# Experts of a mixture-of-experts layer run four at a time in column tiles, their tokens fetched as rows from DRAM

## The chip, the core and the metric

The kernel runs on one core of one Trainium2 chip. The core has a matrix engine (TensorE, "PE" in the profile, with its weight loads as "PEld"), a vector engine ("DVE"), a scalar engine ("ACT"), GpSimd ("POOL") and a sync engine ("SP") that mostly issues DMAs. All data are 32-bit floats. The metric is the device time of one execution in microseconds (us), as the median of several runs.

## The reference

Two transformer-like blocks run over 512 tokens of 1024 columns. The last part of the second block, the only one that the change touches, is a hierarchical mixture of experts: each token chooses one of 8 groups and in it 2 of 8 experts. Cut to what matters:

```python
x = x + merged @ w_out
h2 = rms_norm(x, norm2_g).reshape(b * s, d)
...
expert_id = g_sel[:, None] * 8 + top_i                 # two experts of 64 for each token
gate = p_group[:, None] * jax.nn.softmax(top_v, axis=-1)
...
def expert_block(args):                                 # d_model 1024, d_ff 256
    xb, e = args
    hid = jax.nn.silu(xb @ w_gate_e[e]) * (xb @ w_up_e[e])
    return hid @ w_down_e[e]
...
return x + jnp.zeros_like(h2).at[tok].add(ys * wt[:, None])
```

There are 1024 assignments of a token to an expert, and each expert's three matrices are 1 MiB each, 192 MiB for all 64.

## The kernel before

The two blocks up to the output projection are one long stream of dense products on PE; they end near 1590 us and are the same in both kernels. What follows is the expert part, in this order in the program.

*Routing.* `ev_out2` runs once for each of four blocks of 128 tokens: it adds the output projection to x (kept in four tiles `xt[m]`, token rows), takes the row's 1/rms, transposes the block for the router's logits and ranks the tokens within their experts (`Rk`: the place of a token in its expert's list, or a negative number). Each expert has a block of 32 token places (CAP); two experts with more than 32 tokens are put last and get a second block each (N_SPARE = 2). Any further ones would follow in a loop, which makes no pass with these inputs. The tokens of the first four experts are collected within `ev_out2` already, by products with one-hot columns added up in two banks that `gather_open` sets to zero: a memset on POOL (L1582) and a product of it on PE (tile `xqT<-zero`).

*Weights.* `load_w` loads one matrix into one slab of 1 MiB by one DMA from SP (L1859). There are 16 slabs; `pump_w(limit)` issues loads ahead until `limit` slabs are in use, and `drop_w` gives a slab back. The limit is 13 for the first two experts, then 12, then 11, since the sums (`acc`) take two slabs. The matrices of one expert lie in the buffers of the dense products' pieces. From expert 24 on the order of the experts is found at run time.

*Fetching tokens.* For each group of 8 experts `select` and `gates` build one-hot matrices (token, place) `S` and the same times the gates, `gate_rows` brings the gates along a row, and `gather_k` multiplies x with `S` on PE, in 8 chunks of 4 products, giving the tokens transposed (`xsT`, 1024 columns on partitions, 256 places). ACT and DVE evict the chunks in turn.

*One expert.* `gate_up` runs 16 products of 128x32 by 128x256 in four column tiles of PE (two halves of K, gate and up) and ACT copies the 128x256 result (`part`). `hidden` adds the halves and transposes by two products with a constant "i2"; ACT takes a tanh, DVE three small products (L2062 to L2064, the last one with the row of gates). `down` runs 8 products of 128x32 by 128x256, four column tiles for four quarters of the output. `expert_out` brings the four quarters to their places: four ACT copies (L2086, the high part) and four DVE subtractions (L2088, the low part), 32x256 each.

*Adding up.* For each four experts `scatter_mat` builds a one-hot (place, token) matrix `ST` (DVE `sel` L2105, one product, DVE L2109) and `combine` multiplies it with the high and low parts of the output, 8 times 2 products of 512 columns, and DVE adds each to `acc` (L2123). After the last group each half block is stored by SP (L2343).

*Order.* All engines run in program order. A table in the code (`todo`, `early`, filled by `at`) says ahead of which expert each step of fetching, scattering and adding is emitted, so that PE has such work between the products of an expert that depend on each other. All products are recorded at the helper's line, L114, and the shape of the tiles tells them apart. An instruction of PE shows as two records where the data are 32-bit (16 products of `gate_up` as x32).

Of the kernel before, what the change touches and what calls it, by code (L numbers as in the profile page):

```python
# [10 lines left out]
F32 = mybir.dt.float32  # L11
# [9 lines left out]
P = 128  # L21
T = 512
# [14 lines left out]
def const_arrays():  # L37
    """Constants that follow from the shapes."""
# [15 lines left out]
    i2 = np.zeros((P, P))  # L54
    for r in range(P):
        i2[r, r % 64] = 1.0
    add("i2", i2)
# [22 lines left out]
def layer_kernel(ctx, tc, A, out, dbg=None, stop=None):  # L80
# [96 lines left out]
    def rsqrt_steps(v, scale, res):  # L177
        """Steps towards two [P, 1] factors (appended to res) whose product is scale/sqrt(v)."""
# [13 lines left out]
    def alternate(*lists):  # L192
        """Run the steps of some chains in turn."""
# [5 lines left out]
    def split(hi, lo, src, scale=None):  # L199
        """src (f32) as the exact sum of two float32r tiles."""  # L200
# [7 lines left out]
    def split_later(hi, lo, src, scale=None, lag=0):  # L208
        """split, the engines' parts emitted one after the other."""
# [14 lines left out]
    class Pair:  # L224
        """hi/lo slabs of an activation laid out [128, kc, n]; chunks from `extra` on lie in m2 tiles."""
# [20 lines left out]
    class Ref:  # L246
        """Stands for a Pair that is made later."""

    def diag(r, r2=None):
        """diag(r), or diag(r * r2)."""  # L250
# [7 lines left out]
    def scaled(xap, f):  # L258
        """Rows times their two factors, in place."""
# [6 lines left out]
    def sum_squares(xh):  # L266
        """Sums of squares of the rows of some halves of 512."""
# [6 lines left out]
    def rstd_steps(xh, res, ss=None):  # L274
        """Steps towards two factors of 1/rms of the rows given as two halves of 512."""
# [77 lines left out]
    class Step:  # L353
        """run() emits the products, yielding after each few (a piece when it is done with that one)."""
# [9 lines left out]
    def ws_steps(wap, K, c0, ncols, ref, evac):  # L364
        """out^T tiles [128 columns, T] of pair^T @ w[:, c0:c0+ncols]; evac(j, ps)."""
# [39 lines left out]
    def xs_steps(wap, c0, ref, nm_blocks, evac):  # L405
        """out [128 tokens, 512] of pair @ w[:, c0:c0+512], K = 1024; evac(m, ps)."""
# [24 lines left out]
    def narrow_step(wap, c0, ref, evac):  # L431
        """out^T [32, T] of pair^T @ w[:, c0:c0+32], K = 1024."""
# [15 lines left out]
    def full_steps(wap, K, ref, evac, hold=True):  # L448
        """out [T tokens, 1024] of pair @ w; evac(m, [ps0, ps1]). Uses every PSUM bank."""
# [40 lines left out]
        if hold:  # L490
            # the third block's evacuation waits until the next weights are under way
# [49 lines left out]
    def pump_lows(upto=None):  # L541
        """Emit the low parts of pieces prepared in an earlier quantum, and all up to piece `upto`."""
# [33 lines left out]
    def run_steps(n, rate=0.0):  # L576
        """Emit the next n dense steps, with `rate` background ticks per 24 products."""
# [41 lines left out]
    def pipeline(units):  # L619
        """units: lists of (lag in quanta, function); one unit starts per tick."""  # L620
# [1796 lines left out]
```

## Time and profile before

| | |
|---|---|
| runs, us | 2151.99, 2151.8, 2159.45 (median 2151.99) |
| profiled execution, span | 2155.4 us, 31387 instructions |
| its own time | no other than its span is given; the span is 3.4 us above the median |
| PE busy | 2063.3 us (96%) |
| DVE / ACT / POOL busy | 1251.3 (58%) / 839.4 (39%) / 83.9 (4%) |
| first expert's product to the end | 1608.3 to 2155.4 us |

The profile page gives busy time per engine over the whole span, then the span in 40 slices of 53.9 us. The change touches only what lies behind about 1570 us, that is the last 11 slices, so the whole-span shares say little about it; windows, waits and the timeline of that part say more. "Busy" of PE is modelled from the ends of matmuls. The granted clock of TensorE is given as a share of its full 2.4 GHz; 0.5 is the lower level.

### The profile page before, as it was taken

The numbers are of one execution on the slowest core, as the hardware profiler recorded it, in microseconds if no ns is written. First come the engines' busy times: TensorE is split into PE (matmuls) and PEld (weight loads), VectorE is DVE, ScalarE is ACT, GpSimd is POOL, SyncE is SP. The second block draws the span as 40 slices with busy tenths as digits, with TensorE's granted clock in tenths as the row PEclk, the third lists the DMA queues.
The fourth block names the chain that finished last, engine by engine and source line by source line (L and its number), as shares of the span: only waits on it lengthen the run. The fifth ranks groups of instructions, "written<-read, shape, count | busy, mean of one in ns | idle before, by whom it ended". The sixth has DMA issues, their size and how long they took to land.

```text
span 2155.4 us, 31387 instructions
## 1 busy us (share of the span) xinstructions
PE 2063.3 (96%) x12321; PEld 1611.6 (75%) x12322; DVE 1251.3 (58%) x2820; ACT 839.4 (39%) x1747; POOL 83.9 (4%) x94
## 2 busy tenths in 40 slices
PE   7999999999999999989999999999999889989996
PEld 6777788888888888766687888888887656657664
DVE  5445436437665623878755887584354555665555
ACT  5443323325444422535533655552213333333322
POOL 3000000001000000211010000000000000000000
PEclk9999999999999999999999999999999999999998
DMA  9522232354112352301113242342747999999992
GB/s 229 192 84 69 79 98 79 108 176 157 45 54 78 132 191 88 110 20 42 54 45 127 89 137 79 108 116 90 256 170 271 346 391 372 418 389 368 418 378 98
DMA packets 164406, 363.59 MB, mean 169 GB/s; under 512 B 17706, under 2 KB 116338, under 8 KB 140064
## 3 DMA queue, kind: packets, MB, share of 16 engines
q1 hardware_dynamic: 157536, 341.31, 43.6%
q0 software_dynamic: 6720, 20.25, 3.4%
q8 instruction: 98, 1.61, 0.3%
q14 instruction: 52, 0.43, 0.1%
HBM read 355.15 MB, written 9.00 MB: 169 GB/s over the span
## 4 chain that ended last, share of the span: by engine, by line
PE 65%; DVE 8%; ACT 2%; issue 1%; ACTq 0%; POOL 0%; POOLq 0%
PE ws L114 30%; PE full L114 7%; PE xsT L114 6%; PE gu L114 5%; PE down L114 3%; PE xs L114 3%; PE cmb L114 2%; PE xqT L114 1%; DVE ys L2088 1%; PE hid L114 1%; PE yps L114 1%; DVE acc L2123 1%; ACT ys L2086 1%; PE o L114 1%; PE ssc L114 1%
## 5 line engine op out<-in xcount | busy, mean ns | idle before, releaser
L114 PE MATMUL ws<-hTh,wh 128*128 128x512 f32 x1152 | 467.6, 406 | 0.5 <-ACT q2T L1073 0.5
L346 DVE TENSOR_TENSOR wl<-raw,wh 128x1024 fp32r<-128x1024 f32 x230 | 283.8, 1235 | 308.2 <-ACT wh L339 306.7
L114 PE MATMUL ws<-hTh,wl 128*128 128x512 f32 x1152 | 449.5, 390 | 0.0
L114 PE MATMUL ws<-hTl,wh 128*128 128x512 f32 x1152 | 449.4, 390 | 0.0
L339 ACT ACTIVATE wh<-raw 128x1024 fp32r<-128x1024 f32 x247 | 259.1, 1053 | 233.0 <-PE ws L114 106.5
L114 PEld LDWEIGHTS ws<-hTh,wh 128*128 128x128 f32 x1152 | 216.3, 188 | 63.0 <-issue 17.7
L114 PEld LDWEIGHTS ws<-hTh,wl 128*128 128x128 f32 x1152 | 216.2, 188 | 46.8
L114 PEld LDWEIGHTS ws<-hTl,wh 128*128 128x128 f32 x1152 | 216.6, 188 | 42.9 <-issue 2.2
L691 DVE SCALAR_TENSOR_TENSOR cv<-ws,pcol,cv 128x510 f32<-128x510 f32 (+1 forms) x152 | 113.8, 749 | 115.7 <-ACT cv L689 112.6
L2088 DVE TENSOR_TENSOR ys<-down,ys 32x256 fp32r<-32x256 f32 x264 | 111.0, 421 | 114.8 <-ACT ys L2086 111.8
L2086 ACT ACTIVATE ys<-down 32x256 fp32r<-32x256 f32 x264 | 98.8, 374 | 191.8 <-PE down L114 189.3
L114 PE MATMUL xsT<-S,x 128*128 128x256 f32 (+2 forms) x512 | 139.3, 417 | 0.8 <-ACT S L1969 0.8
L114 PEld LDWEIGHTS xsT<-S,x 128*128 128x128 f32 x512 | 126.9, 334 | 13.0 <-issue 8.9
L114 PE MATMUL gu<-we,xsT 128*32 128x256 f32 x1856 | 117.7, 397 | 0.0
L114 PE MATMUL cmb<-ys,ST 128*128 128x512 f32 x264 | 95.2, 458 | 5.0 <-DVE ys L2088 3.5
L114 PEld LDWEIGHTS gu<-we,xsT 128*32 128x32 f32 x1856 | 64.3, 115 | 43.9 <-issue 8.9
L114 PE MATMUL down<-we,hid 128*32 128x256 f32 x1056 | 75.2, 407 | 21.9 <-DVE hid L2064 15.6
L2123 DVE TENSOR_TENSOR acc<-acc,cmb 128x512 f32<-128x512 f32 x120 | 80.6, 684 | 25.2 <-PE cmb L114 23.9
L689 ACT ACTIVATE cv<-ws,pcol 128x512 f32<-128x512 f32 x64 | 49.7, 776 | 108.6 <-PE ws L114 108.6
L114 PEld LDWEIGHTS down<-we,hid 128*32 128x32 f32 x1056 | 29.5, 113 | 56.7 <-DVE hid L2064 21.2
L114 PE MATMUL xs<-wh,hTh 128*128 128x512 f32 x160 | 66.2, 414 | 1.8 <-ACT wh L339 1.7
L114 PE MATMUL xs<-wl,hTh 128*128 128x512 f32 x160 | 64.0, 400 | 2.6 <-DVE wl L346 2.6
(544 smaller groups left out, 3284.9 us busy)
## 6 DMA issues: line engine op xcount, KB each, us to landing
we<-in_w_gate_e SPq DMA_DIRECT2D x63, 1024.0 KB, 10.2
we<-in_w_up_e SPq DMA_DIRECT2D x63, 1024.0 KB, 8.6
we<-in_w_down_e SPq DMA_DIRECT2D x63, 1024.0 KB, 9.9
raw<-in_w_in SPq DMA_DIRECT2D x56, 1024.0 KB, 5.3
raw<-in_w_up SPq DMA_DIRECT2D x22, 1024.0 KB, 5.2
raw<-in_w_down SPq DMA_DIRECT2D x11, 1024.0 KB, 6.4
raw<-in_w_out SPq DMA_DIRECT2D x8, 1024.0 KB, 4.9
AC<-acum_d POOLq DMA_DIRECT2D x16, 512.0 KB, 4.9
```

The costliest lines, as they stand in the source:

```text
L114: pe.matmul(o, l, r, start=start, stop=stop)
L339: act.activation(hi, src, AF.Copy)
L346: eng.tensor_tensor(lo, src, hi.bitcast(F32), op=ALU.subtract)
L689: act.activation(a, src, AF.Identity, scale=taps[0], bias=bias)
L691: dve.scalar_tensor_tensor(a[:, lag:], src[:, :T - lag], taps[lag], a[:, lag:], op0=ALU.mult, op1=ALU.add)
L2086: act.activation(hi[32 * j:32 * j + 32, a], dp[32 * q:32 * q + 32, :], AF.Copy)
L2088: dve.tensor_tensor(lo[32 * j2:32 * j2 + 32, a], dp[32 * q:32 * q + 32, :], hi[32 * j:32 * j + 32, a].bitcast(F32), op=ALU.subtract)
L2123: dve.tensor_tensor(o_, o_ if gs[0] else xt[m][:, c], ps, op=ALU.add)
```

## The change

Routing, ranking, the weights and the arithmetic of the experts stay. What is different:

- `ev_out2` also stores each block of x to a third DRAM tile, by a DMA from POOL.
- The experts go in groups Q of four (15 of four, one of two, and one with two blocks for each of the last two experts). `pair` does gate and up of two experts in the four column tiles, all eight parts of K in one sum; `hidden` transposes with two products per pair and does not multiply by gates; `down` runs four experts in the four column tiles, 16 products of 512 columns into two banks.
- `group_out` evicts 128 rows at once, two ACT and two DVE instructions of 512 columns, with the gate as a scale for each row.
- The tokens of the next group are fetched as rows: `slots` builds the one-hot of 4 x 32 places, `table` gets gate, token number and 1/rms for each place by four products of 6 columns and four small DVE operations, `fetch` issues an indirect DMA from POOL with the token numbers (an empty place has a number out of range and is skipped), and `turn` scales the rows on ACT, transposes them with eight products and evicts them by one DVE and four ACT instructions.
- `combine` adds into the tiles of x, so `acc` is gone and 13 slabs are for weights throughout. The three matrices of expert 3 (not 1) lie in the buffers of the pieces. The order of the weights is gate and up of two experts, gate and up of the next two, then the four down matrices.
- The table of the order is replaced by one loop over the groups.

```diff
     def ev_out2(m, pss):
...
         for x_, p_ in zip(xh, pss):
             dve.tensor_tensor(x_, x_, p_, op=ALU.add)
+        gp.dma_start(x_d[2][m * P:(m + 1) * P, :], xap)
...
-    E_SMALL, N_FIRST = 1, 10
-    w_order = [(e, i) for e in range(last[0]) for i in range(3) if e != E_SMALL]
...
+    E_SMALL, N_FIRST, N_LIVE = 3, 10, 13
+    w_order = []
+    for e in range(0, N_EXP, 2):
+        w_order += [(e + j, i) for j in range(2) for i in range(2)]
+        if e >= 4 * N_Q:
+            w_order += [(e + j, 2) for j in range(2)]
+        elif e % 4:
+            w_order += [(e - 2 + j, 2) for j in range(4)]
...
+    def table(Q):
+        w_, S = width(Q), sel_S[Q]
+        tp = bank((P, 6), "tab")[0:w_]
+        for m in range(NM):
+            mm(tp, S[:, m, :], Gx[:, m, min(Q, N_Q), :], start=m == 0, stop=m == NM - 1)
...
+    def fetch(Q):
+        w_ = width(Q)
+        xg[Q] = pieces.tile([P, D], F32, tag="wh", name=nm("xg"))[0:w_]
+        gp.indirect_dma_start(out=xg[Q], out_offset=None, in_=x_d[2],
+                              in_offset=bass.IndirectOffsetOnAxis(ap=slot[Q][2], axis=0),
+                              bounds_check=T - 1, oob_is_err=False)
+
+    def turn(Q):
+        w_, x_ = width(Q), xg.pop(Q)
+        act.activation(x_, x_, AF.Copy, scale=slot[Q][1])
+        t = pieces.tile([P, 8, w_], F32, tag="wl", name=nm("xT"))
+        for b in range(2):
+            ps = bank((P, 4, w_), "xT")
+            for k in range(4):
+                pe.transpose(ps[:, k, :], strided(x_, 4 * b + k), ident[0:w_, 0:w_])
...
-    def gate_up(xc, wts):
+    def gate_up(xcs, wts):
         gu = bank((P, 256), "gu")
-        for k4 in range(4):
-            for q in range(4):
-                kh, ch = q // 2, q % 2
-                k = 4 * kh + k4
-                mm(gu[32 * q:32 * q + 32, :], xc(k), wts[ch](k), start=k4 == 0, stop=k4 == 3)
+        for k in range(8):
+            for q in range(4):
+                mm(gu[32 * q:32 * q + 32, :], xcs[q // 2](k), wts[q](k), start=k == 0, stop=k == 7)
...
-    def down(hid, wd):
-        dp = bank((P, 256), "down")
-        for f in range(2):
-            for q in range(4):
-                mm(dp[32 * q:32 * q + 32, :], hid[:, f, :], wd(f)[:, 256 * q:256 * q + 256],
-                   start=f == 0, stop=f == 1)
-        return dp
+    def down(hids, wds):
+        dps = [bank(name="down") for _ in range(2)]
+        for h in range(2):
+            for f in range(2):
+                for j, wd in enumerate(wds):
+                    mm(dps[h][32 * j:32 * j + 32, :], hids[j // 2][:, f, j % 2, :], wd(f)[:, h * T:(h + 1) * T],
+                       start=f == 0, stop=f == 1)
+        return dps
...
+    for Q in range(N_Q + 1):
+        whole = Q < N_Q
+        part = pair(Q, 0, 4 * Q)
+        ready(Q + 1)
+        if Q == 0:
+            rank_cols()
+            table(0)
+        else:
+            combine(Q - 1, range(2))
+        hids = [hidden(part)]
+        if whole:
+            part = pair(Q, 2, 4 * Q + 2)
...
+        if Q:
+            combine(Q - 1, range(2, NM))
+        scatter_mat(Q)
+        if whole:
+            hids.append(hidden(part))
+        turn(Q + 1)
+        second(Q, hids, [4 * Q + j for j in range(4 if whole else 2)])
```

(`ready` is slots, table and fetch of a group; `second` is down and `group_out`; `pair` and `second` give back their slabs and issue further loads.)

PE late in the expert part, from the last combining products ahead of an expert's down to it. In a row stand the line, the operation, the output and the operands. Before, one expert:

```order
L114 MATMUL cmb_16973<-ys_16541,ST_16693 128x512
L114 MATMUL cmb_16973<-ys_16542,ST_16693 128x512
L114 MATMUL hid_16977<-ca,part_16958 128x128 x2
L114 MATMUL xsT_16985<-S_16439,x_12143 128x128 x2
L114 MATMUL xsT_16985<-S_16442,x_12144 128x128 x2
L114 MATMUL cmb_17001<-ys_16541,ST_16693 128x512
L114 MATMUL cmb_17001<-ys_16542,ST_16693 128x512
L114 MATMUL ST_17005<-RkT_13656,sel_17006 128x512
L114 MATMUL down_17011<-we_16733,hid_16980 32x256 x8
```

After, a group of four experts, ending with the first five of 16 down products:

```order
L113 MATMUL cmb_13730<-ys_13586,ST_13530 128x512
L113 MATMUL cmb_13730<-ys_13587,ST_13530 128x512
L113 MATMUL ST_13735<-RkT_13293,sel_13736 128x512
L2023 MATMUL hid_13740<-ca,part_13708 128x128 x2
L1992 MATMUL xT_13749<-ca,xg_13648 128x128 x4
L1992 MATMUL xT_13755<-ca,xg_13648 128x128 x4
L113 MATMUL down_13764<-we_13512,hid_13671 32x512
L113 MATMUL down_13764<-we_13578,hid_13671 32x512
L113 MATMUL down_13764<-we_13580,hid_13743 32x512
L113 MATMUL down_13764<-we_13582,hid_13743 32x512
L113 MATMUL down_13764<-we_13512,hid_13671 32x512
```

Before, fetching and combining products stand between an expert's hid and its down; after, the transposes of the next group's fetched rows (xg) stand there, and the down products read the hid of both pairs.

POOL from the start of routing (x_12144 and x_12145 are the tiles of two token blocks each, x_d_93 the third DRAM tile). Before:

```order
L1828 MEMSET routing_12149 128x8x24
L1833 DMA routing_12149<-in_norm_g 128x8
L1582 MEMSET zero_12601 128x512
L2195 MEMSET ov_15528 128x2
L2346 TENSOR_LOAD nx_15562
```

After:

```order
L1826 MEMSET routing_12150 128x8x24
L1831 DMA routing_12150<-in_norm_g 128x8
L1535 DMA x_d_93<-x_12144 128x1024 x2
L1535 DMA x_d_93<-x_12145 128x1024 x2
L1580 MEMSET zero_12606 128x512
L1980 DMA xg_12803<-x_d_93,ix_12798 128x1024
L1980 DMA xg_12983<-x_d_93,ix_12978 128x1024
```

The memset for the zero product now stands behind four stores of x, and the fetches of the groups (16 in all) behind it.

DVE late in the expert part. Before, what stands in a row for one expert:

```order
L2105 CAST sel_17494<-ca 64x128
L2109 TENSOR_SCALAR ST_17497<-ST_17493,ca 128x512
L2088 TENSOR_TENSOR ys_17509<-down_17499,ys_17508 32x256 x4
L2062 SCALAR_TENSOR_TENSOR hid_17540<-hid_17540,hid_17537 128x64
L2063 TENSOR_TENSOR hid_17540<-hid_17540,hid_17537 128x64
L2064 TENSOR_TENSOR hid_17540<-hid_17540,grow_17174 128x64
L2123 TENSOR_TENSOR acc_13245<-acc_13245,cmb_17545 128x512
```

After, from the second pair's hid of one group to the slot operations of the next:

```order
L2027 SCALAR_TENSOR_TENSOR hid_13539<-hid_13539,hid_13536 128x128
L2028 TENSOR_TENSOR hid_13539<-hid_13539,hid_13536 128x128
L1994 TENSOR_TENSOR xT_13544<-xT_13545,routing_12150 128x512
L2054 SCALAR_TENSOR_TENSOR ys_13587<-down_13560,slot_13210,ys_13586 128x512
L2054 SCALAR_TENSOR_TENSOR ys_13587<-down_13561,slot_13210,ys_13586 128x512
L1958 TENSOR_TENSOR S_13635<-routing_12150,ca 128x512
L1969 TENSOR_TENSOR slot_13642<-tab_13637,ca 128x4
L1970 TENSOR_REDUCE slot_13642<-slot_13642 128x1
L1972 TENSOR_SCALAR ix_13643<-tab_13637 128x1
L1973 COPY slot_13642<-tab_13637 128x1
```

Four evictions per expert have become two per four experts, and the numbers of the rows to fetch (ix) come out of four small operations that stand behind the one-hot S.

## Rows read from the trace of the kernel before

**Rows 1.** The page: span; busy us, share, instructions; GB/s of 40 slices.

```profile
span 2155.4 us, 31387 instructions
...
PE 2063.3 (96%) x12321; PEld 1611.6 (75%) x12322; DVE 1251.3 (58%) x2820; ACT 839.4 (39%) x1747; POOL 83.9 (4%) x94
...
GB/s 229 192 84 69 79 98 79 108 176 157 45 54 78 132 191 88 110 20 42 54 45 127 89 137 79 108 116 90 256 170 271 346 391 372 418 389 368 418 378 98
```

**Rows 2.** Windows: us, busy of PE PEld DVE ACT POOL, clock, DMA share, GB/s.

```profile
1620.00:1660.00 40.00, 39.18 (x346) 31.70 (x349) 17.90 (x49) 13.11 (x36) 0.00 (x0) 1.00 0.70 263
...
1820.00:1860.00 40.00, 38.05 (x347) 28.17 (x347) 20.79 (x52) 13.29 (x37) 0.00 (x0) 1.00 1.01 418
```

**Rows 3.** Waits from 1620 (PE) and 1500 (SP): waiter, releaser, sum us, count, longest.

```profile
PEld down L114 <- DMA we<-in_w_up_e: 1.0, 4, 0.2
...
PE down L114 <- DVE hid L2064: 15.6, 13, 3.9
...
SPq L1859 <- PE down L114: 288.9, 59, 9.9
SPq L1859 <- PE gu L114: 105.7, 60, 19.3
```

**Rows 4.** Groups by form from 1620 us: busy us, mean ns, then idle before.

```profile
L2088 DVE TENSOR_TENSOR ys<-down,ys 32x256 fp32r<-32x256 f32 x264 | 111.0, 421 | 114.8 <-ACT ys L2086 111.8
L114 PE MATMUL xsT<-S,x 128*128 128x256 f32 x384 | 105.6, 419 | 0.8 <-ACT S L1969 0.8
...
L2123 DVE TENSOR_TENSOR acc<-acc,cmb 128x512 f32<-128x512 f32 x120 | 80.6, 684 | 25.2 <-PE cmb L114 23.9
...
L114 PE MATMUL hid<-ca,part 128*128 128x128 f32 x260 | 43.8, 292 | 0.6 <-ACT part L2050 0.6
```

**Rows 5.** The chain that ended last: start us, length us, engine, work, records.

```profile
1571.20 0.88 PE h2T L1520 x8
...
1774.20 1.86 PE down L114 x16
...
1790.46 1.07 PE down L114 x16
1791.53 1.73 PE gu L114 x32
...
2113.91 1.85 PE cmb L114 x8
```

**Rows 6.** Timeline from the routing to the first experts: start, length, engine, instruction, [idle before].

```profile
1567.15 0.52 POOL L1582 MEMSET zero<- 128x512 bf16 x1 [38.95 <-issue]
...
1588.17 0.39 PE L114 MATMUL xqT<-zero,routing 128*128 128x512 bf16 x1
...
1589.13 1.28 DVE L1535 TENSOR_TENSOR x<-x,full 128x512 f32<-128x512 f32 x2
...
1608.34 4.52 PE L114 MATMUL gu<-we,xqT 128*32 128x256 f32 x64
...
1611.16 0.33 SPq L1859 DMA_DIRECT2D we<-in_w_up_e  x1
```

**Rows 7.** DMA issues: count, KB each, us from issue to landing.

```profile
we<-in_w_down_e SPq DMA_DIRECT2D x63, 1024.0 KB, 9.9
...
dsk<-in_d_skip POOLq DMA_DIRECT2D x2, 4.0 KB, 18.6
```

**Rows 8.** Timeline of SP at the end: the last weights and the stores of the output.

```profile
2100.63 2.04 SPq L1859 DMA_DIRECT2D we<-in_w_down_e  x2
...
2137.16 7.70 SPq L2343 DMA_DIRECT2D out<-acc  x8
```

**Rows 9.** A window with a low clock, and the ST product in it and later.

```profile
1770.00:1780.00 10.00, 7.73 (x58) 3.67 (x58) 5.60 (x14) 2.15 (x7) 0.00 (x0) 0.66 0.99 401
...
1773.44 0.76 PE L114 MATMUL ST<-RkT,sel 64*128 64x512 f32 x1 [2.27 <-DVE sel L2105]
...
1833.98 0.49 PE L114 MATMUL ST<-RkT,sel 64*128 64x512 f32 x1 [1.34 <-DVE sel L2105]
```

More of the change, by code (lines that the diff above doesn't have):

```diff
@@ L53, in const_arrays @@
     add("swa", np.where(np.concatenate([prev_ok, own_ok], 1), 0.0, 8.0 * NEG))
[L54 to L57, printed above, removed]
+    add("m4", 0.5 * (p[:, None] // 32 == np.arange(4)[None, :]))
+    add("m2", 0.5 * (2 + p[:, None] // 32 % 2 == np.arange(4)[None, :]))
     add("iota32", np.broadcast_to(np.arange(32), (P, 32)))
@@ L743, in pairs_of @@
         return [t[j] for i in range(0, len(lists[0]), 2) for t in lists for j in (i, i + 1) if j < len(t)]
-    x_d = [drp.tile([T, D], F32, name=f"x_d{i}") for i in range(2)]
+    x_d = [drp.tile([T, D], F32, name=f"x_d{i}") for i in range(3)]
     nxt = {}
@@ new lines, in slots @@
+    def slots(Q):
+        S = sel_S[Q] = m2((P, NM, width(Q)), name="S")
+        n = 4 if Q < N_Q else 2
+        e0 = 4 * Q if Q <= N_Q else N_EXP - N_SPARE
+        sh = [P, NM, n, CAP]
+        for i in range(1 if Q <= N_Q else 2):
+            s = S.rearrange("p m (r e s) -> p m r e s", e=n, s=CAP)[:, :, i]
+            dve.tensor_tensor(s, Rk[:, :, e0:e0 + n, None].to_broadcast(sh),
+                              C("iota64")[:, None, None, CAP * i:CAP * i + CAP].to_broadcast(sh), op=ALU.is_equal)
@@ L2051, in gate_up, with hidden @@
         return part
-    def hidden(part, gr):
+    def hidden(part):
         cp = bank((P, 2, P), "hid")
@@ L2322, in second_half @@
-    def second_half(e, hid):
-        dp = down(hid, weights(e, 2))
-        pump_w(limit(e))
-        expert_out(e, dp)
-    part = None
-    for e in range(N_EXP - N_SPARE):
-        this = part or gate_up_of(e)
-        part = gate_up_of(e + 1) if e < N_AHEAD else None
-        second_half(e, first_half(e, this))
-    hids = []
-    for e in range(N_EXP - N_SPARE, N_EXP):
-        two = [(b, gate_up_of(b)) for b in (e, e + N_SPARE)]
-        hids += [(b, first_half(b, part)) for b, part in two]
@@ L2336, in layer_kernel, with xcol @@
-    for b, hid in hids:
-        second_half(b, hid)
-    assert not todo and not early
-    for m in range(NM):
-        for h in range(2):
-            c = slice(h * T, (h + 1) * T)
-            combine([G4 - 1, G4], m, h)
-            sp.dma_start(out[0, m * P:(m + 1) * P, c], acc[m // 2][:, m % 2, c])
+    group_gates()
+    group_tokens()
+    sel_S[0] = moe["q"][0][0]
+    order, prep = order_prep(), overflow_prep()
+    def xcol(Q, j):
+        return lambda k: xT[Q][k // 4][:, k % 4, 32 * j:32 * j + 32]
@@ new lines, in pair, with second @@
+    def pair(Q, j, e, last=True):
+        part = gate_up([xcol(Q, j), xcol(Q, j + 1)], [ew[e + b, i] for b in range(2) for i in range(2)])
+        if last:
+            for b in range(2):
+                for i in range(2):
+                    drop_w(e + b, i)
+            pump_w(N_LIVE)
+        return part
+    def second(Q, hids, es):
+        dps = down(hids, [ew[e, 2] for e in es])
+        for e in sorted(set(es)):
+            drop_w(e, 2)
+        pump_w(N_LIVE)
+        group_out(Q, dps)
@@ new lines, in ready @@
+    def ready(Q):
+        slots(Q)
+        table(Q)
+        fetch(Q)
+    for Q in range(N_Q + 1):
[5 more added lines that the diff above has]
+            table(0)
+        else:
+            combine(Q - 1, range(2))
+        hids = [hidden(part)]
+        if whole:
+            part = pair(Q, 2, 4 * Q + 2)
+        if Q in (1, 2):
+            next(order, None)
+            next(order, None)
+        if Q in (8, 9, 10, 11):
+            next(prep, None)
+        if Q:
+            combine(Q - 1, range(2, NM))
[4 more added lines that the diff above has]
+        second(Q, hids, [4 * Q + j for j in range(4 if whole else 2)])
@@ L2346, in layer_kernel @@
+    Q, e = N_Q + 1, N_EXP - N_SPARE
+    part = pair(Q, 0, e, last=False)
+    combine(Q - 1, range(2))
+    hids = [hidden(part)]
+    part = pair(Q, 2, e)
+    combine(Q - 1, range(2, NM))
+    scatter_mat(Q)
+    hids.append(hidden(part))
+    second(Q, hids, [e, e + 1, e, e + 1])
+    assert wnext["i"] == len(w_order) and not ew and next(order, None) is None and next(prep, None) is None
+    combine(Q, range(NM), store=True)
     nov = nc.values_load(ov["n"][0:1, 0:1], min_val=0, max_val=MAXBLK)
```

295 lines of the change are left out of this document (84 added, 211 removed).

## The prediction

> **What bounds the kernel now.** I read the page's head, busy shares and GB/s line first [rows 1]: one core, span 2155.4 us, PE 96% busy; only in the last quarter does the GB/s line come up to 418. The experts run from 1608 us to the end, so everything below is about some 547 us. I then cut that part into windows [rows 2]: at 1820 to 1860 the queues carry 418 GB/s at a share of 1.01 and PE is busy for 38 of 40 us; at 1620 to 1660 PE is busy for 39.2 and the queues move only 263 GB/s. Two things are near their end at once, and the waits tell which one paces [rows 3]: PE waited 1.0 us in all for a weight, while the weight queue on SP waited 289 + 106 us for PE's products to leave a slab. So PE paces, and the DMA idles behind it in the parts below 418.
>
> The floor of the other side: 64 experts have 192 matrices of 1 MiB [rows 7]. Sixteen are issued before the first slab is free (13 slabs, three in the buffers of the dense products); the other 176 are 184.5 MB, at 418 GB/s 441.5 us. Before issues them from 1611 to 2102 [rows 6, 8], 491 us: 33.5 us for every twelve, that is for four experts.
>
> **The change part by part.**
>
> *PE, per four experts.* After, gate/up has as many products as before: 4 × 1.73 = 6.9 us at the full clock [rows 5]. Down has half the instructions at twice the width; at equal columns it is the old 4 × 1.07 = 4.3, with 3.5 as the other end if some of the old time was start-up; I take 4. Combining stays 8 × 2 products of 0.23 (eight took 1.85) = 3.7. The one-hot products that fetched tokens go: 105.6 us for the 384 of six groups of eight [rows 4], 8.8 for each four experts; in their place come 8 transposes, 0.88 like the eight h2T [rows 5], 4 table products of 6 columns (a 292-ns hid product is the nearest above [rows 4], so 0.2 to 1.2), an ST of 0.5 [rows 9] and 4 hid transposes below 1.2. Sum about 17 to 18 us; with some 3 us of waits inside (before waited 15.6 us in 13 places for hid [rows 3], 1.2 each; here two hid chains and the turn of the fetched rows) 21, against before's 33.5.
>
> *DVE and ACT, per four.* Before, 16 evictions of 421 ns and 8 adds of 684 [rows 4], the hid operations and part of the token evictions; after, 2 evictions of 512 columns (684 bounds one), 4 hid operations, 8 adds of 684, 4 small slot operations and one 512-wide xT: 11 us on DVE where about 20 stood. ACT falls likewise. Neither nears 30 us.
>
> *DMA, per four.* 12 matrices = 12.58 MB, 30.1 us at 418 GB/s. The fetches are new: 1024 token places less the 47 of the first four experts, by the reference's router, are 977 rows of 4 KB = 4.0 MB, 9.6 us in all if they only take bytes; unused slots are skipped (if they moved bytes as well, 8 MB, 19 us). So a group needs 30.7 us of the queues and 21 of PE: **the queues become the bound**, if the slabs hold enough of a lead. All 13 stay with weights (before: 13, 12, then 11), and nine matrices are in flight or landed while PE works on a pair, 22 us of stream.
>
> *The new wait on POOL.* ev_out2 now stores each x block to DRAM from POOL, ahead of gather_open's memset. Before, the memset ran at 1567.15, long before need, and PE's zero product at 1588.17 [rows 6]. Now it is queued behind the last block's store, which waits for the DVE adds ending 1590.4; the issue is put at 0.5, as long as the memset's 0.52, so PE's zero product stands at about 1591.5: 3.3 us later, on the path, with the routing behind it. The lower bound is 0 (if routing's other chain hides it), the upper 4. I take 3.3. The last store's half MB is 1.3 us of the queues at 418 GB/s, and the weights' queue stands still until 1611 [rows 6], so that costs nothing; under a full stream it would cost those 1.3.
>
> *The sum.* First gate/up 1608.3 + 3.3 = 1611.6; two experts 4.5 at the clock found there, so the first slabs are free at 1616.2. A gap while the first groups run through their lead: 0 to 8 us, since the lead covers 22; I take 0. Stream 441.5 + fetch 9.6 + 2 for the last landing: last weight at 2069 to 2070. After it, PE has the second pair's gate/up, combining and hid of the last four blocks partly undone: last down lands some 5 us after the last gate/up; from then gate/up 3.45 × 2, combining 1.85 × 2, hid chain 2 to 3 put the down at T + 8.5, its 4 us, 2.2 for evictions, 8 adds of 0.684 to T + 20, and from the last store's issue to the end 10.5 as before (2144.9 to 2155.4 [rows 8]): T + 31. Before took 52.7 us from its last weight's issue to the end [rows 8], and its queues stood empty for most of it. End: 2070 + 31 = 2101 of span, against 2155.4: −54.7. The profiled execution is 3.4 us above the median of 2151.99; taken off, **2097 us**.
>
> **The rivals.**
>
> A, above: the queues set the pace. For it: 418 GB/s holds over 40 us while PE computes [rows 2], and in two slices of 54 us of the page [rows 1]. Bounds: no fetch cost, 3.3 hidden, and a tail of 25 give 2079; a starting gap of 8, every row moved and a tail at half clock (+7) give 2112.
>
> B, the clock. In A, PE idles 10 us in 31, in gaps before each pair and each down. The rows show what a gap does: after 2.27 us idle the ST product of 64 x 512 took 0.76, and 16 down products 1.86, against 1.07 later; the window's clock was 0.66 [rows 5, 9]. After 1.34 us idle the same ST took 0.49 [rows 9]. At half clock a group needs 34 to 37 us, more than the stream; but then the gaps close and the clock comes back (before runs at 1.00 with few gaps), so I expect 31.5 to 34 per group: 15 × 0.8 to 3.3 more, 2109 to 2147. The Trainium skill, "TensorE: Matmul & The Clock Gate", HAM oscillation, describes just this: compute shorter than the wait for the next transfer starts every burst cold; held to the letter, all groups at 37 would end near 2192, but such groups leave no gap.
>
> C, the stream is slower than 418. The page's slices from 1670 us to the last two lie at 346 to 418 [rows 1], with PE pacing; rows fetched at scattered addresses may cost more than their bytes. At 372, 188.5 MB take 507, not 451: 2153, **no change**. The Trainium skill, "DMA: Bandwidth & Descriptors", Specifications, gives an HBM limit of about 358 GB/s per core: by it the stream would take 527 and the end be near 2172. The trace disagrees with 418 [rows 1, 2].
>
> D, slower: the fetch's latency. Indices for group Q+1 are ready only after PE's table products in group Q, and turn, before Q's down, needs the rows; PE's down is queued behind turn. The slowest POOL transfers of the trace, two small ones, took 18.6 us [rows 7]. With F from index to landing, a group cannot be shorter than F and what lies on that circle besides: scaling the rows 1, transposes 0.9, their evictions 2, down 4, the next gate/up 3.5, table and slot operations 1.2, in all 12.6 + F. It sets the pace from F = 18.1; 15 groups reach before's time at 2097 + 15 × (12.6 + F − 30.7) = 2152, F = 21.8, and at F = 23 the time is 2171. Against it: the fetches have a queue of their own, and 9.9 for a 1 MiB weight in the full stream [rows 7] shows how little waits there.
>
> **How the numbers follow.** A 0.66 (2079 to 2112), B 0.18, C 0.08, D 0.08. The likeliest is A at 2097. To leave out 2 in 10, the range goes over A and most of B: 2078 to 2133. A difference of 0.5% (10.8 us) is about what a measurement of this kernel can tell from none. Faster by more: A, nearly all of B (below 2141) 0.16, 0.02 of C: 0.84. Same: 0.02 of B, 0.05 of C: 0.07. Slower: D and a rest of C: 0.09.
>
> **What would show it.** Right: windows of the middle groups at 410 or more GB/s, PE near 70% busy with waits on "we" DMAs, the queues never empty although SP still waits for PE to leave slabs (they are refilled as they come free), groups 31 us apart, the memset behind the x_d stores at 1591. B shows as granted clock well below 1 with groups above 32. C shows as DMA share 1.0 with fewer GB/s. D shows as PE waiting at xT for ACT and that for xg. Wrong altogether if down in four column tiles takes much more than 4 us, or the tail more than 40.

## The result, and the profile after

The changed kernel takes 2124.64 us (median of 4 runs, 2123.8 to 2126.57); the kernel before, over the runs made by then, 2154.82. The ratio is 0.9858 (95% interval 0.9839 to 0.9877): 1.4% faster. The forecast was 2097 us with a range of 2078 to 2133. The way it went is case A, the queues set the pace; the gain is 30 us where 55 were worked out, and the time lies above case A's own bounds (2079 to 2112).

The page of the changed kernel, the lines that answer to [rows 1] and [rows 7]:

```profile
span 2124.8 us, 28524 instructions
...
PE 1963.7 (92%) x11203; PEld 1472.0 (69%) x11204; DVE 1130.5 (53%) x2456; ACT 751.0 (35%) x1457; POOL 102.4 (5%) x114
...
GB/s 217 205 89 67 83 88 73 88 198 139 74 65 80 70 227 90 122 21 21 62 70 107 116 96 90 100 100 119 122 248 286 415 419 419 420 419 420 416 414 81
...
q0 software_dynamic: 9520, 26.29, 4.2%
...
we<-in_w_down_e SPq DMA_DIRECT2D x63, 1024.0 KB, 20.4
```

The GB/s line now stands at 414 to 420 in eight slices in a row, where before it went up and down between 346 and 418. A weight takes 20.4 us from issue to landing, not 9.9: 20.4 us x 419 GB/s is 8.2 matrices, so eight loads are under way at a time. The same in windows of 100 us (columns as in [rows 2]):

```profile
1640.00:1740.00 100.00, 81.38 (x762) 46.26 (x755) 43.44 (x105) 18.06 (x40) 4.01 (x4) 0.89 1.01 416
1740.00:1840.00 100.00, 76.68 (x633) 38.63 (x631) 32.83 (x70) 17.15 (x39) 3.00 (x3) 0.87 1.01 419
1840.00:1940.00 100.00, 72.77 (x617) 37.24 (x620) 37.07 (x99) 15.49 (x35) 3.10 (x4) 0.83 1.01 420
```

PE is busy 73 to 81% of the time at a mean clock of 0.83 to 0.89, and the DMA share is 1.01 throughout. The waits (from 1600 us for PE, 1500 for SP; columns as in [rows 3]) have changed sides:

```profile
PEld gu L113 <- DMA we<-in_w_up_e: 52.1, 28, 2.4
...
PE xT L1992 <- ACT xg L1987: 29.1, 16, 5.3
...
SPq L1857 <- DMA we<-in_w_down_e: 100.5, 50, 3.2
...
SPq L1857 <- PE down L113: 54.0, 12, 14.5
```

PE now waits for weights, and the weight queue waits mostly for its own transfers and little for PE's slabs (before, 289 + 106 us for PE). The groups keep step with the fetches on POOL, the second and the last of the 16:

```profile
1644.47 1.02 POOL L1980 DMA_INDIRECT xg<-x_d,ix  x1 [21.83 <-PE cmb L113]
...
2073.24 1.01 POOL L1980 DMA_INDIRECT xg<-x_d,ix  x1 [32.54 <-DVE x L2082]
```

Between them lie 14 groups, 428.8 / 14 = 30.6 us each on average (30.7 forecast; single groups take 27 to 34).

Where the start and the end differ from the sum is seen on PE's timeline (start, length, instruction, [idle before]):

```profile
1591.00 0.39 PE L113 MATMUL full<-wh,mgpl 128*128 128x512 f32 x1
1594.88 0.38 PE L113 MATMUL xqT<-zero,routing 128*128 128x512 bf16 x1 [3.49 <-POOL zero L1580]
...
1615.11 4.15 PE L113 MATMUL gu<-we,xqT 128*32 128x256 f32 x64
...
1631.87 1.97 PE L1992 MATMUL xT<-ca,xg 128*128 128x128 f32 x8 [5.34 <-ACT xg L1987]
1633.77 5.04 PE L113 MATMUL down<-we,hid 128*32 128x512 f32 x32
...
2064.60 6.36 PE L113 MATMUL gu<-we,xT 128*32 128x256 f32 x58 [1.86 <-DMA we<-in_w_up_e]
...
2082.83 1.97 PE L1992 MATMUL xT<-ca,xg 128*128 128x128 f32 x8 [4.14 <-ACT xg L1987]
...
2102.08 3.63 PE L113 MATMUL down<-we,hid 128*32 128x512 f32 x28 [1.33 <-DVE hid L2028]
```

And three windows, the dip after the first wait for fetched rows and the emptying of the queues:

```profile
1630.00:1635.00 5.00, 3.13 (x16) 1.97 (x20) 0.69 (x1) 2.27 (x5) 0.00 (x0) 0.50 1.01 421
1635.00:1640.00 5.00, 5.00 (x56) 1.66 (x52) 1.06 (x2) 1.40 (x3) 0.00 (x0) 0.84 0.40 133
...
2076.00:2080.00 4.00, 0.50 (x1) 0.18 (x1) 2.89 (x7) 0.00 (x0) 0.00 (x0) 1.00 0.42 173
```

By bytes the stream ends at 2077 (2060 to 2080 carries 338 GB/s, 16 us of a full one, and the next 20 us under 1 more); the end of the span is 2124.8, 48 us later. The prediction's 31 us counted from the landing of the last weight, though. SP issued that one at 2064.67, the second of the two here, and the last line is its time to landing:

```profile
2062.19 2.82 SPq L1857 DMA_DIRECT2D we<-in_w_down_e  x2
...
DMA to landing us min/median/max: 19.8/19.8/19.8
```

So it landed at 2084.5, and the tail counted from there is 40 us.

### The profile page after: what moved, and what is told of

The parts are those of the page before. It is cut to its first block, busy times and chain, and to the rows that moved or that the text cites. A ratio compares the mean times of both kernels' runs of the same rounds, so it can differ in the third digit from the quotient of the medians.

```text
span 2124.8 us, 28524 instructions
## 1 busy us (share of the span) xinstructions
PE 1963.7 (92%) x11203; PEld 1472.0 (69%) x11204; DVE 1130.5 (53%) x2456; ACT 751.0 (35%) x1457; POOL 102.4 (5%) x114
## 3 DMA queue, kind: packets, MB, share of 16 engines
q0 software_dynamic: 9520, 26.29, 4.2%
HBM read 363.21 MB, written 11.10 MB: 176 GB/s over the span
## 5 line engine op out<-in xcount | busy, mean ns | idle before, releaser
L113 PE MATMUL gu<-we,xT 128*32 128x256 f32 x1984 | 155.2, 416 | 52.0 <-DMA we<-in_w_up_e 36.2
L113 PEld LDWEIGHTS gu<-we,xT 128*32 128x32 f32 x1984 | 72.0, 119 | 132.7 <-DMA we<-in_w_up_e 52.1
L2082 DVE TENSOR_TENSOR x<-x,cmb 128x512 f32<-128x512 f32 x136 | 84.7, 681 | 49.3 <-PE cmb L113 48.1
L113 PE MATMUL down<-we,hid 128*32 128x512 f32 x528 | 85.1, 754 | 1.3 <-DVE hid L2028 1.3
L2015 ACT ACTIVATE part<-gu 128x256 f32<-128x256 f32 x33 | 12.7, 384 | 194.7 <-PE gu L113 194.7
L113 PE MATMUL cmb<-ys,ST 128*128 128x512 f32 x264 | 72.0, 415 | 0.4 <-DVE ys L2054 0.3
L2054 DVE SCALAR_TENSOR_TENSOR ys<-down,slot,ys 128x512 fp32r<-128x512 f32 (+1 forms) x34 | 25.5, 750 | 84.9 <-ACT ys L2051 84.0
L113 PE MATMUL xs<-wh,hTl 128*128 128x512 f32 x160 | 64.2, 401 | 1.1 <-DVE hTl L307 1.1
L113 PE MATMUL full<-wh,fh 128*128 128x512 f32 x160 | 62.3, 390 | 0.0
L113 PE MATMUL full<-wh,fl 128*128 128x512 f32 x160 | 62.2, 389 | 0.0
## 6 DMA issues: line engine op xcount, KB each, us to landing
we<-in_w_gate_e SPq DMA_DIRECT2D x63, 1024.0 KB, 19.8
we<-in_w_up_e SPq DMA_DIRECT2D x63, 1024.0 KB, 19.8
we<-in_w_down_e SPq DMA_DIRECT2D x63, 1024.0 KB, 20.4
```

Source lines behind the costliest of these rows:

```text
L113: pe.matmul(o, l, r, start=start, stop=stop)
L2015: act.activation(part, gu, AF.Copy)
L2054: dve.scalar_tensor_tensor(lo[0:w_, c], ps[0:w_], g, hi[0:w_, c].bitcast(F32), op0=ALU.mult, op1=ALU.subtract)
L2082: dve.tensor_tensor(xt[m][:, c], xt[m][:, c], ps, op=ALU.add)
```

## The experiments

All but one start from the changed kernel, and so do their diffs. A ratio, with its 95% interval, stands against runs of the kernel before made beside it; gains and losses in us are against the changed kernel's median of 2124.6. Times with an interval are medians of four runs, the others single runs.

**Does the stream set the pace?** Four runs.

*Fewer weights.* 26 matrices less, all products kept:

```diff
-    w_order = [w_ for w_ in w_order if w_[0] != E_SMALL]
+    w_order = [w_ for w_ in w_order if w_[0] != E_SMALL and (w_[1] < 2 or w_[0] % 2 == 0 or w_[0] < 8 or w_[0] >= 4 * N_Q)]
...
-        dps = down(hids, [ew[e, 2] for e in es])
+        dps = down(hids, [ew[e, 2] if (e, 2) in ew else ew[e - 1, 2] for e in es])
...
```

> The changed kernel, but 26 of the 192 weight matrices are not loaded: from expert 9 to 59 every second expert uses the down matrix of its neighbour. All products stay. Theory A (the queues set the pace between 1640 and 2077 us): 26 x 2.5 us = 65 us less, near 2060, and the DMA stays full. Theory B (PE at its lowered clock sets the pace and the full queues only look so): 0 to 10 us less.

2059.19 us, 65.4 less than the changed kernel; the 26 matrices take 65.1 at 419 GB/s. (Counted from the last dense product to the end, the two profiles differ by 68, so that it fits so closely is luck.) The queues stay full (the window of the middle):

```profile
1740.00:1840.00 100.00, 76.60 (x698) 42.30 (x690) 43.15 (x113) 15.68 (x36) 4.09 (x5) 0.89 1.01 419
```

*The same in the kernel before*, with 27 matrices less:

```diff
-    w_order = [(e, i) for e in range(last[0]) for i in range(3) if e != E_SMALL]
+    w_order = [(e, i) for e in range(last[0]) for i in range(3) if e != E_SMALL and (i < 2 or e % 2 == 0 or e < 8)]
...
```

> The kernel before the change, with 27 of the 192 weight matrices not loaded (from expert 9 on every second expert uses the down matrix of its neighbour). All products stay. Theory (PE paced the kernel before, the queues had room): 0 to 10 us less, since the queues were full in places (1820 to 1900 us). Rival (the queues set the pace of the kernel before as well): 27 x 2.5 = 68 us less.

2152.82 us, against 2154.18 (2152.73 to 2157.66) for the kernel before beside it: nothing. The queues just carry less while PE goes on at its pace:

```profile
1740.00:1840.00 100.00, 89.12 (x815) 62.35 (x816) 58.91 (x150) 33.93 (x94) 0.00 (x0) 0.97 0.86 329
```

So 27 MB are worth 65 us after the change, and 28 MB nothing ahead of it. That is the whole change in one pair of runs: the bound moved from PE to the queues.

*More work for PE.* 16 products of 128x512 in each group behind scatter_mat:

```diff
         scatter_mat(Q)
+        if Q:
+            extra = bank(name="extra")
+            for i in range(16):
+                mm(extra, STs[Q - 1][:, 0:P], STs[Q - 1], start=i == 0, stop=i == 15)
```

> The changed kernel, with 16 more products of 128x512 in each group but the first (15 groups, 0.23 us each at the full clock, 3.7 us a group), whose result is not used. Theory A: they fall into PE's waits, and the only cost is in the last group, after the last weight: 0 to 5 us more, 2125 to 2130, with a higher granted clock in the middle. Theory B: PE paces, 15 x 3.7 = 55 us more, near 2180.

2121.64 us (ratio 0.9832, 0.9815 to 0.9848; its interval overlaps that of the changed kernel, so the 3 us less are not shown to be real). Some 56 us of work cost nothing, and the granted clock rose to 0.93 to 0.98 in the windows where the changed kernel had 0.83 to 0.89:

```profile
1801.92 3.93 PE L113 MATMUL extra<-ST 128*128 128x512 f32 x16
...
1808.57 3.64 PE L113 MATMUL down<-we,hid 128*32 128x512 f32 x32
```

Behind the added products the 32 down records took 3.64 us; in the changed kernel the down of the same group took 5.50 (at 1803.51), with the same wait of 1.40 us for the fetched rows a little ahead of it in both, and 5.04 in the first group (above). So the gaps do lower the clock, as case B said, and in the middle groups it does not matter for the time.

*Much more work for PE.* 48 in place of 16.

> The changed kernel with 48 more products of 128x512 in each group but the first, 11.5 us a group at the full clock; the one-hot fetching products of the kernel before were 8.8 us for four experts. Theory: PE's own work is 21 us a group at the full clock, with these 32.8 against 30.9 of the queues, so PE becomes the bound again and gives 15 x 1.9 = 28 us more, near 2150, the clock near 1.0 and the queues below 418 GB/s. Rival 1 (the waits inside a group take the products in): 0 to 10 more. Rival 2 (PE's clock stays low): 15 x 11.5 = 170 more.

2167.7 us, 43 more than the changed kernel, 18 more than expected: neither the theory's number nor a rival's. The middle of it:

```profile
1740.00:1840.00 100.00, 91.84 (x819) 61.26 (x811) 32.53 (x69) 16.01 (x35) 3.00 (x3) 1.00 0.98 403
1840.00:1940.00 100.00, 85.43 (x670) 58.85 (x670) 34.68 (x95) 13.62 (x33) 3.10 (x4) 0.95 0.91 376
```

PE is the bound again. Its plain groups take 31.5 us (fetches at 1747.79, 1779.36, 1810.92), better than the 32.8 expected; 11.2 of that are the added products, so PE's own group is 20 us. But five groups take 32 to 41, those in which the order of the experts (38.0, 35.2) and the overflow blocks (41.1, 32.1, 36.4) are prepared; in the changed kernel the same groups take 27 to 33. These are serial chains: a PE with slack hides them, a PE without it adds them. The point from which PE takes over lies between 4 and 11.5 us of added work per group, and the fetching products of before were 8.8 [rows 4].

**What do the fetched rows cost?**

```diff
-            dve.tensor_scalar(ix, tp[:, 4:5], float(N_AWAY), None, op0=ALU.add)
+            dve.tensor_scalar(ix, tp[:, 4:5], float(2 * N_AWAY), None, op0=ALU.add)
```

> The changed kernel, but every row number is out of range, so that the 16 fetches are issued, wait and land without moving rows (the experts then work on what lies in the buffers). Theory A: the rows take the bytes' time of the full queues, 4.0 MB / 419 GB/s = 9.5 us, and their landing in the first and last groups some 4 us each: 10 to 18 us less, 2107 to 2115. Rival (fetched rows cost more than their bytes; the page's HBM reads grew by 8.1 MB, not 4): 20 us or more. Rival D (fetch latency paces every group): 15 x 5 us, 2050 or less.

2107.25 us (0.977, 0.9754 to 0.9786): 17.4 less. In its profile the software queue moved 22.30 MB, not 26.29: 3.99 MB of rows, 9.5 us at 419 GB/s. Where the 17.4 lie:

```profile
2047.22 5.26 PE L113 MATMUL gu<-we,xT 128*32 128x256 f32 x58 [1.86 <-DMA we<-in_w_up_e]
...
2063.41 1.97 PE L1992 MATMUL xT<-ca,xg 128*128 128x128 f32 x8 [3.20 <-ACT xg L1987]
...
2060.00:2080.00 20.00, 16.80 (x169) 9.14 (x168) 6.95 (x12) 4.70 (x10) 0.00 (x0) 0.83 0.22 91
```

PE's last wait for a weight ends 434.3 us after the first expert's product began (1612.97); in the changed kernel it is 449.5 (1615.11 to 2064.60), so 15.2 lie in the stream. Behind that wait 58.1 us follow, not 60.2: the last fetch's wait is 3.20 for 4.14, and the gate/up runs at a higher clock (5.26 for 6.36). Of the 15.2, some 10 are bytes: by bytes the stream ends at 2064.3 (the last line). The rest is the landing of the last weights: issued at 2047.30 and landed 19.8 us later, the last one comes 2.8 us behind the end by bytes, and with rows it comes 7.5 behind (2084.5 against 2077).

So the rows cost about 15 us of the stream, 9.5 by their bytes and some 5 because the last weights land later behind the bytes; why they do is not shown. The total is the one that theory A expected, but its second term is not: the waits for fetched rows stay (4.75 us in the first group, 5.34 in the changed kernel). The rival was right that rows cost more than their bytes, and wrong by how much. The figure that it went by does not count moved rows: the page's HBM reads (355.15 MB before, 363.21 after) stand at 363.21 without rows as well.

**The start.** The last store put behind the memset:

```diff
-        gp.dma_start(x_d[2][m * P:(m + 1) * P, :], xap)
+        store = lambda: gp.dma_start(x_d[2][m * P:(m + 1) * P, :], xap)
+        if not last:
+            store()
...
         gather_open()
+        store()
```

> The changed kernel, with only the last block's store of x put behind the memset on POOL's queue, so that the memset no longer waits for the last adds. In the changed kernel PE waited 3.49 us for the memset (zero product at 1594.88, 7.8 us after the blocks' stores allow it). Theory: the wait lies on the path to the first expert and all that follows is shifted by it: 3 to 3.5 us less, near 2121. Rival: the routing of the last block (DVE) ends last anyway and takes the place of the wait: 0 to 1 us, 2124.

2120.89 us (0.9826, 0.981 to 0.9842), 3.7 less. The two intervals overlap a little; the trace shows the gain by itself. The zero product now follows the dense ones at once, and the first expert starts 20.4 us behind the last dense product, not 24.1:

```profile
1589.49 0.39 PE L113 MATMUL full<-wh,mgpl 128*128 128x512 f32 x1
1589.72 0.61 PE L113 MATMUL xqT<-zero,routing 128*128 128x512 bf16 x2
```

**Down ahead of turn.** The two calls change places, so that the down products run while the rows are fetched:

```diff
+        second(Q, hids, [4 * Q + j for j in range(4 if whole else 2)])
         turn(Q + 1)
-        second(Q, hids, [4 * Q + j for j in range(4 if whole else 2)])
```

> The changed kernel with turn behind the down products and evictions of its group in place of ahead of them. In the changed kernel PE waited 5.34 us (first group) and 4.14 (last but one) for fetched rows, and behind the first of these waits the weight queue ran dry for some 4 us (133 GB/s at 1635 to 1640). Theory: the fetch's latency costs only at these two places; down goes into both waits and slabs come free earlier at the first: 4 to 8 us less, 2117 to 2121. Rival D (the fetch paces every group): over 20 us less. Rival: the transposes and their evictions now stand between down and the next gate/up of each group and give it back: 0 to 5 more.

2117.72 us (0.983, 0.9814 to 0.9847), 6.9 less. The dip near 1636 is gone and the first down follows its hid:

```profile
1620.00:1640.00 20.00, 17.60 (x205) 9.37 (x197) 7.54 (x17) 4.88 (x11) 1.02 (x1) 1.00 1.01 419
...
1621.80 4.71 PE L113 MATMUL down<-we,hid 128*32 128x512 f32 x32
1628.35 1.16 PE L1992 MATMUL xT<-ca,xg 128*128 128x128 f32 x8 [1.85 <-ACT xg L1987]
```

In its profile PE's last wait for a weight ends 445.4 us after the first expert's product (449.5 before), and 56.2 follow (60.2): 4 us in the stream, 4 at the end. Only these few us, and not 5 in each of 15 groups: the fetch (median 8.5 us to landing, 1.0 of issue) paces none of the middle groups. Case D falls.

**The end.** The last two groups in another order:

```diff
+    part = pair(Q, 0, e)
+    turn(Q + 1)
+    combine(Q - 1, range(2))
+    hid0 = [hidden(part)]
+    part = pair(Q + 1, 0, e + 2, last=False)
+    combine(Q - 1, range(2, NM))
+    scatter_mat(Q)
+    hids = [hidden(part)]
+    part = pair(Q + 1, 2, e + 2)
+    scatter_mat(Q + 1)
+    hids.append(hidden(part))
+    second(Q, hid0, [e, e + 1])
+    second(Q + 1, hids, [e + 2, e + 3, e + 2, e + 3])
...
```

> The changed kernel with another end: in the last two groups (experts 60, 61 and the two with two blocks each) all gate/up products come first, then both down products, the tokens of the last group are fetched one group earlier, the last four down matrices are the last weights, and both groups are added up in one sum and one add. In the changed kernel 48 us lie between the last weight's landing (2077) and the end, where the prediction had 31. Theory: the 17 us are the last groups in series (a fetch of 8.5 us, PE waiting 4.1 for it, two gate/up pairs, two chains of hid behind the last landing), and this order takes away 15 to 20: 2105 to 2110. Rival: what counts is the end itself (evictions, 8 adds, stores, 25 us from the last down), so 0 to 5 less.

2114.55 us (0.9813, 0.9796 to 0.9829): 10 less, where 15 to 20 were expected. The wait for the last fetch shrank to 1.5 us, but PE came to the end late for another reason:

```profile
2064.76 6.22 PE L113 MATMUL gu<-we,xT 128*32 128x256 f32 x58 [1.86 <-DMA we<-in_w_up_e]
...
2083.63 5.34 PE L113 MATMUL gu<-we,xT 128*32 128x256 f32 x64
...
2089.91 7.06 PE L113 MATMUL down<-we,hid 128*32 128x512 f32 x48
...
2099.15 5.09 SPq L2083 DMA_DIRECT2D out<-x  x8
```

From the landing that frees the first of the three pairs (2064.76) PE works with little pause to 2097, some of it at the lower clock (6.22 and 5.34 where 64 records take 3.66). What is left is work, evictions and stores, not waiting. Counted from the landing of the last weight (issued at 2064.83, landed 2084.6) the tail is 31.9 us, near the 31 of the prediction; the 17 us that were to be won held 7.5 us that are the late landing, and this order did not touch that.

*Another end* (with the three savers above): the last four down matrices ahead of the last gate and up.

> As the three together, but with the end the other way: the four down matrices of the last two groups are loaded ahead of the gate and up of the last two experts, experts 60 and 61 are finished and added up while the last four matrices come, and what is left behind the last landing is two gate/up pairs, one hid chain, one down, evictions, 8 adds and stores: 3.7 + 0.4 + 3.7 + 2 + 4.7 + 2.5 + 5.5 + 10.5 = 33 us, where the other order left 39. Theory (the end is PE's work after the last landing): 5 to 6 us less than the three together, 2099 to 2104. Rival (the last weights land later than they would, or PE's low clock stretches the end): as the three together or more, 2106 and above.

2110.59 us (0.9798, 0.9781 to 0.9815): no gain over the run below (3 us more, with overlapping intervals). PE adds up the group before (16 products, 5.64 us) and prepares two scatter matrices ahead of the gate/up of experts 60 and 61, which starts only at 2063.77, 7 us behind the landing of its last weight (2056.4); but the last weight of all landed at 2076.3, and the last gate/up starts at 2076.52:

```profile
2063.77 3.66 PE L113 MATMUL gu<-we,xT 128*32 128x256 f32 x64
...
2076.52 7.11 PE L113 MATMUL gu<-we,xT 128*32 128x256 f32 x128
```

From that landing to the end it is 32 us, near the 33 expected. The 39 of the other order was counted from the end by bytes; from the last landing that order leaves 32 as well (31.9, above).

**All three together.**

> The three changes that took time away, together: the memset ahead of the last store, down ahead of turn, and the end with all gate/up ahead of the last two downs. Theory (each acts at a place of its own: before the first expert 3.7, the dry queue near 1636 some 4, the end 10): 2105 to 2109. Rival (down ahead of turn had its gain at the end as well, where the new order already takes it; or turn between down and the next gate/up costs): 2110 to 2115.

2107.21 us (0.9784, 0.9766 to 0.9802; 2106.8 to 2109.6): as expected, 17.4 us faster than the changed kernel and 2.2% faster than before. One by one the three gave 3.7 + 6.9 + 10 = 20.6. The profiles, cut at the start of the last dense product, the first expert's product, PE's last wait for a weight and the end, show what adds up (us):

| | to the first expert | to the last wait for a weight | to the end |
|---|---|---|---|
| changed kernel | 24.1 | 449.5 | 60.2 |
| last store behind the memset | 20.4 | 450.8 | 60.2 |
| down ahead of turn | 24.3 | 445.4 | 56.2 |
| the other end | 24.2 | 449.3 | 51.7 |
| all three | 20.4 | 445.7 | 51.7 |

The start and the dry queue add up; the 4 us that down ahead of turn gains at the end lie within what the new order gains there. The rival was right in this, and too high in its time.

**The lead of the slabs.** Nine slabs as the limit in the program (`N_LIVE` 9, the first pump 9):

> The changed kernel with 9 slabs for weights, not 13. The prediction named the lead of nine matrices (22 us) as what keeps the queues full. With 9 slabs the lead over the pair in work is 5 matrices, 12.5 us. Theory: PE leaves the slabs of a pair 4 to 6 us after their landing, so 12.5 us are still about enough: 0 to 15 us more, 2125 to 2140. Rival (the lead of 22 us is needed): the queues empty once in each group, 3 us or more, 45 us or more, 2170 and above.

2123.79 us, no change; but this run does not test the lead. The limit sets where a load stands in the program, and the loads still went round 13 buffers. With four slabs really taken away:

```diff
     due(True)
+    held = [slab((P, 2048), name="held") for _ in range(4)]
+    for h in held:
+        gp.memset(h[:, 0:8], 0.0)
     pump_w(N_LIVE)
...
```

> The changed kernel with 9 slabs for weights where it has 13: four slabs are taken by tiles that are kept to the end. (The run with nine slabs as the limit in the program had 13 buffers still in turn, so its loads waited for the same releases as before.) Four matrices fewer are loaded ahead of the first expert, 4 x 2.5 = 10 us of stream. Theory: behind the four matrices in work five are in flight, 12.5 us, and PE leaves a slab 4 to 8 us after its landing, so the queues stay full: 10 us and up to 10 for the last groups, 2133 to 2145. Rival (the lead must be 20 us): the queues run dry in each group, 3 us or more, with the 10 us 2180 and above.

2134.32 us, 9.7 more, the four matrices that are no longer loaded ahead. SP now waits for PE (from 1640 us):

```profile
SPq L1857 <- PE gu L113: 161.9, 28, 10.3
SPq L1857 <- PE down L113: 159.1, 14, 16.0
```

and the 100 us windows still carry 400 to 418 GB/s. A lead of five matrices is nearly enough, so the eleven slabs of before would probably have done as well (not run).

## Why the prediction was right, and by how much it was off

The mechanism was right: the queues became the bound, at the rate and with the time per group that were worked out. The time was 28 us longer than forecast, and that it lies in the range is partly luck. Case A's own upper bound was 2112, and its terms were added up wrongly there (2097 + 8 + 9.4 + 7 make 2121); 2124.6 lies above both. The range reached so far only to take in case B, whose groups of 31.5 us and more did not come.

- *PE's share of a group, 21 us*: held at the full clock (20 us where PE was the bound). gate/up took 3.63 to 3.66 us per pair (2 x 1.73 forecast), the 32 down records 3.62 to 3.64 (3.5 to 4.3 forecast, 4 taken), combining 2.1 per eight (1.85), the eight transposes 1.16 (0.88).
- *The queues' share, 30.7 us*: 30.6. The rate was 416 to 420 GB/s.
- *The memset behind the last store, 3.3 us*: 3.49 of wait, 3.7 in the run without it. The first expert stood 6.8 us later than before, not 3.3, but the unchanged dense products had ended 3.1 later in this execution (1591.00; before, the zero product followed them directly at 1588.17). Over all the runs here the last dense product starts anywhere from 1586.6 to 1591.7.
- *The gap at the start, 0 to 8, taken as 0*: the queues were short by (419 − 133) x 5 / 419 = 3.4 us in one window and 0.5 in the next, so 4. The reason was not a short lead but down, queued on PE behind the wait for the first fetched rows, which kept its slabs; with down ahead of that wait the gap is gone.
- *The landing of the last weight, 2 us behind the stream, and the rows by their bytes alone, 9.6 us*: the last weight came 7.5 us behind the end by bytes, and 2.8 in the run without rows. So the rows had a price in the sum that was some 5 us too low; where it comes from stays open.
- *The tail, T + 31*: this is the step that failed. From the landing of the last weight it was 40.4 us, just over the 40 that the prediction named as a sign of being wrong altogether. The prediction put the last down at T + 8.5; it came 17.6 us behind the landing (2102.08). From there to the end it was 22.7, and 22.5 forecast. So what was wrong is how far PE is when the last weight lands. The prediction counted the last group alone. It left out that the group ahead of it has a single pair: its fetch (issued at 2073.24, 8.3 us) has no second pair to hide behind, PE waits 4.14 us for it, and that group's down, evictions and adds then stand in front of the last pairs. The gaps cost clock there as well: of the gate/up that takes 3.66 us for 64 records, 58 took 6.36. The price of the fetch was named (case D) for a group in the middle, and was not asked where its cover is gone. With the last two groups in another order the tail was 31.9.
- 3.5 (start) + 4 (gap) + 5.5 (landing) + 9.4 (tail) = 22.4 us of the 23.8 between the span of 2124.8 and the sum of 2101; the rest is spread over the stream. (2155.4 less 2101 is 54.4, not the 54.7 written.) The 3.4 us taken off for the median did not come back: the span of the profile after lies at the median of the runs.
- *Case B*: the gaps do lower the granted clock (0.83 to 0.89 as a mean; down 5.50 us, and 3.64 with 16 more products ahead of it), but PE has 10 us of slack in a group, and a lower clock fills them. The Trainium skill, "TensorE: Matmul & The Clock Gate", HAM oscillation, describes bursts that start cold behind each transfer; the trace agrees with that (0.50 in 1630 to 1635, with the 5.34 us wait) and shows that it costs nothing where the transfers set the pace.
- *Case C*: 419 GB/s held for 400 us with fetches among the loads. The limit of 358 GB/s in "DMA: Bandwidth & Descriptors", Specifications, of the Trainium skill did not show on this chip with one core at work.
- One sign was read wrongly in what I wrote to look for: SP still waiting for slabs. With 13 slabs it waits mostly for its own transfers (100.5 + 91.8 + 69.3 us, against 54.0 + 41.5 for PE).

## What to carry to other kernels

When two resources stand near their ends, price both per period, and test the pair by taking bytes from one kernel and from the other: 27 MB less were worth 65 us in one and nothing in the other. Once transfers set the pace, work added to the compute engine is free up to its slack (here 4 us a group were, 11 were not), and so is a lower clock, but only where there is slack: behind the last weight both cost their time. What is left to win lies in the run-in and the run-out, where the covers of the steady state are missing. Go through those two ends step by step as if they were a program of their own: here some 19 of the 55 us worked out were lost there (4 in the first gap, 5.5 by the late landing, 9.4 in the tail), and three small changes of order won 17 back. And say from which event a tail is counted: from the end by bytes this one is 48 us, from the last landing 40, and an experiment planned on the first figure expected more than there was to win.

## What the runs showed of the hardware

- An indirect fetch of up to 128 rows of 4 KB took POOL 1.0 us to issue and landed 8.5 us (median) after the issue in a full stream, while a 1 MiB load of SP's queue beside it took 20: the fetch did not wait behind the eight loads under way. With every row number out of range it still took 7.4.
- The stream does not stop sharply. From 2070 to 2084 us the rate fell slowly from 437 GB/s to 0 (the line below is 2060 to 2090 in 40 steps of 0.75 us), so the last matrix lands some 7 us later than bytes over rate say. At 2076 to 2080 the mean share of the 16 DMA engines is 0.42 at 173 GB/s; 173 / 0.42 = 412, so the engines still at work have their full rate, and the others have run out of work:

```profile
GB/s 437 426 404 437 393 448 415 437 415 393 448 415 437 360 360 382 306 328 262 213 279 284 191 175 164 104 120 115 76 66 33 22 0 0 22 0 0 0 0 0
```

Without fetched rows the last matrix landed 2.8 us behind, not 7.5.
